# Stores of the triangles and of their 16x16 inverses issued by GpSimd's queue instead of SP's, in a two-layer hybrid decoder kernel

## The chip, the cores and the metric

The kernel runs on one core of one Trainium2 chip. The metric is the device time of one execution in microseconds: the median of three runs before the change is 1626.77 us (1626.5 to 1631.62). The profile is of one further execution, which took 1630.86 us; its span from the first to the last instruction is 1629.1 us.

## What is computed

Two decoder layers are run on two groups that share the weights: a prompt of 512 positions and eight samples of 4 positions. The width is 1024. Each layer is

```python
h = rms_norm(x, g_mix_pre)
p_rw, p_s5, p_gdn, p_swa = split_cols(h @ w_in, PROJ_SPLITS)
mix = concat([rwkv7(p_rw), s5(p_s5), gdn(p_gdn), swa(p_swa)]) @ w_out
x = x + rms_norm(mix, g_mix_post)
f = square(relu(rms_norm(x, g_mlp_pre) @ w_up)) @ w_down        # width 4096
x = x + rms_norm(f, g_mlp_post)
```

Two of the four mixers, RWKV-7 and the gated DeltaNet, are linear recurrences with four heads of 64. For the prompt they are done in chunks of 64 positions, and each chunk needs the inverse of a 64x64 unit lower triangle, as the reference writes it for the DeltaNet:

```python
A = where(strict, bc[..., :, None] * decay * einsum('bhtd,bhjd->bhtj', kc, kc), 0.0)
U = triangular_solve(eye + A, rhs, left_side=True, lower=True, unit_diagonal=True)
```

Outputs are the two groups' activations and every mixer's final state.

## The kernel before, in words

**Halves.** All columns (512 prompt positions and 32 sample positions) are cut into two halves, 0 with 256 columns and 1 with 288. `body` runs the stages for one half beside those of the other: while the mixers of one half run, the projection or the MLP of the other half supplies TensorE with large matmuls.

**Weights.** Every weight is read once per half. A weight unit is 128 output columns; `load_part` (L1675 to 1690) loads half a unit, 256 KB, from DRAM into `wraw` (five buffers) on SP's queue, at L1681. ScalarE rounds it to `whi` (L232), VectorE makes the remainder `wlo` (L236), and TensorE runs twelve matmuls on the two (L220). There are 752 such loads.

**Triangles.** A half has 256 prompt positions, so four chunks in each of four heads: 16 triangles of 64x64 for each of the two mixers, held in one tile `lt` of 128 partitions x 8 x 64 (tile class `t` for RWKV, `g` for the DeltaNet in the trace's names). `tri_begin` starts their inversion and `tri_end` ends it; a call handles the 16 triangles of one mixer, one half and one layer, and is called a triangle from here on. There are eight calls, in pairs (RWKV first, then DeltaNet).

`tri_begin` (L274 to 319) works through DRAM, because the 16x16 diagonal blocks must lie in 64 partitions, one block each:

1. two stores of `lt`, 64 partitions each, to a scratch `trsc` (L283), 64 x 8 runs of 64 floats;
2. one load of the diagonal blocks from `trsc` to `g`, tile class `c` (L286), on SP;
3. GpSimd clears a tile and sets its diagonal (L292, 293); VectorE inverts the 64 blocks with some 20 small multiplications and reductions (L300 to 312) and copies the transposed result (L313);
4. for the inverse and its transpose: one store to the DRAM array `diag` (L316), 64 x 16 runs of 16 floats, and two loads, 64 partitions each, into the tiles `t16t` and `t16` (L318), on SP.

`tri_end` then does six groups of 64x64 matmuls on TensorE, beginning with `lt` against `t16` (ps<-t,t for RWKV, ps<-t,g for the DeltaNet), and grows the 16x16 inverses to 64x64.

**Order.** The kernel is written with a tile framework: `TileContext(nc, schedule_with_timeline_sim=True)`. The framework orders the instructions of all engines anew from a simulated timeline and the priorities in `PRIO` (L137), and inserts the semaphore waits. On the chip every queue is then in order: PE (TensorE), DVE (VectorE), ACT (ScalarE), POOL (GpSimd) and SP. An instruction that waits holds back all that stand behind it on its queue. SP issues all the weight loads, the loads and stores of the triangles, of the S5 tables, of the mixers' outputs (`mix`) and of the states. POOL issues the stores of the residual stream (L1672), of the states and of two S5 tables, and computes sums of squares and small copies.

Of the kernel before, what the change touches and what calls it, by code (L numbers as in the profile page):

```python
# [139 lines left out]
class K:  # L140
# [133 lines left out]
    def tri_begin(self, lt, which):  # L274


        nc = self.nc

        blocks = lambda d: d.rearrange("(m r) -> m r", m=64)[:, :1024].rearrange("m (i t) -> m i t", t=64)[:, :, 0:16]
        rows = lambda d, c: d.rearrange("(h c r) -> c h r", h=8, c=2)[c, :, :4096].rearrange("h (i t) -> i h t", t=64)  # L280
        sc = self.t([64 * 1040], "trsc", pool="dram", bufs=2)
        for c in range(2):
            self.nc.sync.dma_start(out=rows(sc, c), in_=lt[64 * c:64 * c + 64])  # L283
        gp = self.w([64, 17, 16], "c1")
        g = gp[:, 0:16]
        self.nc.sync.dma_start(out=g, in_=blocks(sc))  # L286
        t16t, t16, work = (self.w([128, 8, 64], "t2") for _ in range(3))

        tt2 = self.view(work.rearrange("p a b -> p (a b)")[0:64], [64, 2, 16, 16])
        tt = tt2[:, 0]  # L290
        tmp = self.w([64, 16, 16], "c1")
        nc.gpsimd.memset(tt, 0.0)  # L292
        nc.gpsimd.memset(tt.rearrange("p a b -> p (a b)")[:, ::17], 1.0)

        d8 = lambda a: (a.rearrange("p a b -> p (a b)")[:, 0:272].rearrange("p (h r) -> p h r", h=2)[:, :, 0:128]
                        .rearrange("p h (c j) -> p h c j", c=8)[:, :, :, 0:8])
        t8, g8 = d8(tt2.rearrange("p x c j -> p (x c) j")), d8(gp)
        tm8 = tmp.rearrange("p a b -> p (a b)")[:, 0:128].rearrange("p (h c j) -> p h c j", h=2, c=8)
        for r in range(1, 8):
            self.tt(tm8[:, :, 0:r, 0:r], t8[:, :, 0:r, 0:r],  # L300
                    g8[:, :, 0:r, r].unsqueeze(2).to_broadcast([64, 2, r, r]))
            self.red(t8[:, :, 0:r, r], tm8[:, :, 0:r, 0:r], negate=True)

        ww = self.w([64, 8, 8], "c0")
        t4 = tmp.rearrange("p a b -> p (a b)").rearrange("p (c i j) -> p c i j", c=4, i=8)
        for c in (0, 4):
            self.tt(t4, tt[:, c:c + 4, 0:8].unsqueeze(2).to_broadcast([64, 4, 8, 8]),
                    g[:, 0:8, 8:16].rearrange("p j i -> p i j").unsqueeze(1).to_broadcast([64, 4, 8, 8]))
            self.red(ww[:, c:c + 4], t4)
            self.tt(t4, ww[:, c:c + 4].unsqueeze(2).to_broadcast([64, 4, 8, 8]),  # L310
                    tt[:, 8:16, 8:16].rearrange("p i r -> p r i").unsqueeze(1).to_broadcast([64, 4, 8, 8]))
            self.red(tt[:, c:c + 4, 8:16], t4, negate=True)
        nc.vector.tensor_copy(tt2[:, 1].rearrange("p j c -> p c j"), tt)  # L313
        for x, t in enumerate((t16t, t16)):
            d = self.diag[which][x]
            self.nc.sync.dma_start(out=blocks(d), in_=tt2[:, x])  # L316
            for c in range(2):
                self.nc.sync.dma_start(out=t[64 * c:64 * c + 64], in_=rows(d, c))  # L318
        return lt, t16, t16t, work
# [1741 lines left out]
```

## Time and profile before

| what | value |
|---|---|
| median of 3 runs | 1626.77 us |
| profiled execution / its span | 1630.86 / 1629.1 us |
| PE busy | 1555.1 us (95%) |
| DVE busy | 1195.3 us (73%) |
| ACT busy | 961.8 us (59%) |
| POOL busy | 318.0 us (20%) |
| packets of SP's queue (q1) / of POOL's (q0) | 199180 / 3744 |

Busy time is the time in which an engine executes an instruction; an engine's waits are told by another view, by line, by what released it, in total, in number and the longest. DMAs appear twice: as the time that the issuing queue needs for the instruction, and as the time from issue to landing.

### The profile page before, as it was taken

The page shows a single profiled execution, that of the slowest core. Times are in us where ns is not written, and L with a number is a line of the kernel's source. Part 1 is how long each engine was busy: PE and PEld are TensorE (multiplying, and loading weights), DVE is VectorE, ACT ScalarE, POOL GpSimd, SP SyncE. Part 2 cuts the span into 40 slices and gives each one's busy share as a digit, 9 for nine tenths or more (in the row PEclk, how much of TensorE's full clock was granted, in tenths as well). Part 3 has the DMA queues.
Part 4 walks back from the last instruction along what each step waited for, and adds up shares of the span by engine and source line. Part 5 has one row for each costly group of instructions (what it writes and reads, how often), then busy time and mean ns, then how long its engine had stood idle before and what let it go on. Part 6 is the DMA issues. An engine that isn't in the chain of part 4 may idle for free. (4 is left out here: it accounts for less than half of the span.)

```text
span 1629.1 us, 38773 instructions
## 1 busy us (share of the span) xinstructions
PE 1555.1 (95%) x14528; PEld 1453.4 (89%) x14528; DVE 1195.3 (73%) x2843; ACT 961.8 (59%) x2086; POOL 318.0 (20%) x618
## 2 busy tenths in 40 slices
PE   7989989899999999899999999999999999999996
PEld 7978978689889999888989999989888889999996
DVE  6898786976876867787595567879679755856665
ACT  6766648643455567765454467886444556755544
POOL 4751251000310428100020002620013001200001
PEclk9999999999999999999999999999999999999998
DMA  7645444443566565535365555535436655655552
GB/s 232 200 114 136 143 134 148 109 130 114 173 211 201 171 204 204 182 112 139 105 217 173 167 161 197 180 109 151 138 121 208 205 193 185 210 189 166 163 170 101
DMA packets 203112, 267.38 MB, mean 164 GB/s; under 512 B 81114, under 2 KB 95772, under 8 KB 202508
## 3 DMA queue, kind: packets, MB, share of 16 engines
q1 hardware_dynamic: 199180, 249.94, 48.9%
q0 software_dynamic: 3744, 14.96, 2.5%
q8 instruction: 114, 1.87, 0.5%
q14 instruction: 74, 0.61, 0.1%
HBM read 237.95 MB, written 28.58 MB: 164 GB/s over the span
## 5 line engine op out<-in xcount | busy, mean ns | idle before, releaser
L232 ACT CAST whi<-wraw 128x512 fp32r<-128x512 f32 x752 | 462.6, 619 | 419.2 <-PE ps L220 264.7
L236 DVE TENSOR_TENSOR wlo<-wraw,whi 128x512 fp32r<-128x512 f32 x752 | 534.9, 716 | 209.2 <-ACT whi L232 188.0
L220 PE MATMUL ps<-h,whi 128*128 128x288 f32 (+1 forms) x3264 | 519.5, 297 | 8.4 <-ACT h L228 4.4
L220 PEld LDWEIGHTS ps<-h,whi 128*128 128x128 f32 x3264 | 451.3, 191 | 25.8 <-ACT h L228 6.0
L220 PE MATMUL ps<-f,whi 128*128 128x288 f32 (+1 forms) x2752 | 421.9, 292 | 5.9 <-ACT whi L232 5.8
L220 PEld LDWEIGHTS ps<-f,whi 128*128 128x128 f32 x2752 | 372.0, 189 | 17.1 <-ACT whi L232 7.4
L220 PE MATMUL ps<-h,wlo 128*128 128x288 f32 (+1 forms) x1632 | 285.9, 295 | 5.4 <-DVE wlo L236 5.1
L220 PEld LDWEIGHTS ps<-h,wlo 128*128 128x128 f32 x1632 | 235.8, 191 | 12.3 <-DVE wlo L236 7.8
L220 PE MATMUL ps<-f,wlo 128*128 128x288 f32 (+1 forms) x1376 | 235.8, 292 | 1.7 <-DVE wlo L236 1.7
L220 PEld LDWEIGHTS ps<-f,wlo 128*128 128x128 f32 x1376 | 195.9, 189 | 5.3 <-DVE wlo L236 2.9
L236 POOL TENSOR_TENSOR sums<-sums,d 128x288 f32<-128x288 f32 (+1 forms) x54 | 51.2, 948 | 519.0 <-ACT d L228 517.7
L220 PE MATMUL ps<-r,r 64*64 64x64 f32 (+7 forms) x1184 | 67.8, 236 | 12.7 <-POOL r L236 3.8
L236 DVE TENSOR_TENSOR acc<-acc,ps 128x256 f32<-128x256 f32 (+1 forms) x96 | 41.7, 435 | 49.8 <-PE ps L220 49.7
L220 PEld LDWEIGHTS ps<-r,r 64*64 64x64 f32 (+4 forms) x1184 | 55.9, 140 | 23.2 <-issue 5.9
L232 ACT CAST f<-d 128x288 fp32r<-128x288 f32 (+1 forms) x128 | 53.3, 417 | 35.3 <-DVE d L236 35.3
L228 ACT ACTIVATE d<-ps 128x288 f32<-128x288 f32 (+1 forms) x152 | 59.8, 393 | 8.1 <-PE ps L220 6.1
L236 DVE TENSOR_TENSOR f<-d,f 128x288 fp32r<-128x288 f32 (+1 forms) x128 | 56.7, 443 | 7.4 <-ACT f L232 7.4
L236 DVE TENSOR_TENSOR d<-d 128x288 f32<-128x288 f32 (+1 forms) x128 | 56.7, 443 | 0.0
L228 ACT ACT_TABLE_LOAD x43 | 55.2, 1283 | 0.8
L220 PEld LDWEIGHTS ps<-t,t 64*64 64x64 f32 x1024 | 32.5, 135 | 4.7 <-issue 1.1
L220 PE MATMUL ps<-t,t 64*64 64x64 f32 x1024 | 36.3, 220 | 0.3 <-DMA t<-diag 0.2
L232 ACT COPY r<-ps 64x128 f32<-64x128 f32 (+2 forms) x56 | 20.4, 369 | 26.4 <-PE ps L625 11.6
(404 smaller groups left out, 1851.6 us busy)
## 6 DMA issues: line engine op xcount, KB each, us to landing
wraw<-in_w_up SPq DMA_DIRECT2D x256, 256.0 KB, 2.8
wraw<-in_w_down SPq DMA_DIRECT2D x256, 256.0 KB, 2.9
wraw<-in_w_in SPq DMA_DIRECT2D x176, 256.0 KB, 3.0
wraw<-in_w_out SPq DMA_DIRECT2D x64, 256.0 KB, 3.2
t<-diag SPq DMA_DIRECT2D x32, 128.0 KB, 3.2
x<-acc POOLq DMA_DIRECT2D x3, 1152.0 KB, 6.8
x<-acc POOLq DMA_DIRECT2D x3, 1024.0 KB, 6.4
xs<-mix SPq DMA_DIRECT2D x8, 288.0 KB, 2.9
```

The source lines that it names most:

```text
L220: return self.nc.tensor.matmul(out=out, lhsT=lhsT, rhs=rhs, start=start, stop=stop)
L228: return self.nc.scalar.activation(out=out, in_=in_, func=func, scale=scale, bias=bias, **kw)
L232: return self.nc.scalar.copy(out, in_)
L236: return (eng or self.nc.vector).tensor_tensor(out=out, in0=a, in1=b, op=op)
```

## The change

In `tri_begin`, both kinds of stores are issued by GpSimd's queue. The loads that read them back (L286, L318) stay on SP. That is 32 DMAs of an execution: 16 at L283 and 16 at L316.

```diff
         sc = self.t([64 * 1040], "trsc", pool="dram", bufs=2)
         for c in range(2):
-            self.nc.sync.dma_start(out=rows(sc, c), in_=lt[64 * c:64 * c + 64])
+            self.nc.gpsimd.dma_start(out=rows(sc, c), in_=lt[64 * c:64 * c + 64])
         gp = self.w([64, 17, 16], "c1")
...
             d = self.diag[which][x]
-            self.nc.sync.dma_start(out=blocks(d), in_=tt2[:, x])
+            self.nc.gpsimd.dma_start(out=blocks(d), in_=tt2[:, x])
             for c in range(2):
```

## Rows read from the trace of the kernel before

**Rows 1.** The page's first part: busy us, share of the span, instructions
```profile
PE 1555.1 (95%) x14528; PEld 1453.4 (89%) x14528; DVE 1195.3 (73%) x2843; ACT 961.8 (59%) x2086; POOL 318.0 (20%) x618
```
**Rows 2.** Busy by stretch: bounds, length, five engines, PE clock, DMA share, GB/s
```profile
95.00:165.00 70.00, 64.39 (x663) 56.50 (x663) 60.27 (x200) 44.76 (x130) 17.81 (x47) 0.93 0.49 129
295.00:360.00 65.00, 58.37 (x630) 48.41 (x630) 55.49 (x166) 38.12 (x94) 1.90 (x4) 0.97 0.48 126
715.00:775.00 60.00, 59.55 (x661) 53.34 (x660) 48.13 (x158) 33.49 (x89) 0.00 (x0) 1.00 0.56 149
1110.00:1170.00 60.00, 59.80 (x697) 54.34 (x697) 48.11 (x150) 33.55 (x90) 0.55 (x1) 1.00 0.60 162
```
**Rows 3.** Waits of SP's queue, whole span: total us, times, longest us
```profile
SPq L1681 <- DVE wlo L236: 704.8, 489, 6.1
...
SPq L316 <- DVE t L248: 31.4, 7, 11.8
...
SPq L318 <- DMA diag<-t: 11.1, 11, 2.8
SPq L283 <- DVE t L236: 10.4, 4, 6.4
```
**Rows 4.** ScalarE's waits on weight DMAs, third and fourth stretch (715, 1110)
```profile
ACT whi L232 <- DMA wraw<-in_w_up: 1.8, 1, 1.8
...
ACT whi L232 <- DMA wraw<-in_w_down: 2.3, 3, 1.5
```
**Rows 5.** TensorE's waits for split weights, whole span
```profile
PE ps L220 <- ACT whi L232: 8.1, 8, 2.9
PE ps L220 <- DVE wlo L236: 6.8, 12, 1.7
```
**Rows 6.** The tile trsc: issue ns min/median/max, first and last start
```profile
L283 SPq DMA_DIRECT2D trsc<-t x8: 596/624/628, 103.3 to 1114.3; - x8
```
**Rows 7.** The tile diag, the same columns
```profile
L316 SPq DMA_DIRECT2D diag<-t x16: 574/596/1430, 126.4 to 1156.8; - x16
L1842 POOL DMA_DIRECT2D diag<-r x4: 539/540/582, 69.9 to 71.6; - x4
```
**Rows 8.** DMA issues: queue, count, KB each, median us to landing
```profile
trsc<-t SPq DMA_DIRECT2D x8, 128.0 KB, 2.7
...
diag<-t SPq DMA_DIRECT2D x16, 64.0 KB, 2.8
...
out_swk_p<-sx POOLq DMA_DIRECT2D x2, 64.0 KB, 1.9
...
out_rw_p<-rwS POOLq DMA_DIRECT2D x4, 32.0 KB, 4.6
```
**Rows 9.** Line L1206 on POOL, issue ns min/median/max
```profile
L1206 POOL DMA_DIRECT2D out_swk_s<-c x2: 680/683/686, 495.9 to 1311.6; - x2
```
**Rows 10.** TensorE in order of time: first uses of inverses
```profile
133.57 0.33 PE L220 MATMUL ps<-t,t 64*64 64x64 f32 x2
...
164.48 0.73 PE L220 MATMUL ps<-t,g 64*64 64x64 f32 x17
...
327.64 0.33 PE L220 MATMUL ps<-t,t 64*64 64x64 f32 x2 [0.16 <-DMA t<-diag]
```
**Rows 11.** VectorE's waits for the read-back, third and fourth stretch
```profile
DVE c L236 <- DMA c<-trsc: 2.2, 1, 2.2
...
DVE c L236 <- DMA c<-trsc: 1.7, 1, 1.7
```
**Rows 12.** SP's queue in order of time: start us, us, line
```profile
128.89 2.86 SPq L318 DMA_DIRECT2D t<-diag  x4
...
299.22 1.29 SPq L283 DMA_DIRECT2D trsc<-t  x2
```
**Rows 13.** POOL in order of time, idle time before it and its releaser
```profile
309.78 0.90 POOL L1672 DMA_DIRECT2D x<-acc  x1 [16.22 <-ACT f L228]
```
**Rows 14.** Line L313, ns min/median/max
```profile
L313 DVE COPY t<-t x8: 374/382/395, 127.6 to 1156.1; 64x256 f32<-64x256 f32 x8
```

## The prediction

> **What bounds the kernel now.** I read the page's first part, then the four stretches in which triangles are inverted, then the waits of SP's queue, then who waits on what those queues carry. TensorE is busy for 1555.1 of 1629.1 us [rows 1], so it is the bound, and a change counts only by what it does to TensorE's 74 idle us. There are eight triangles, in four pairs (one RWKV, one DeltaNet each), and the pairs lie in the stretches 95 to 165, 295 to 360, 715 to 775 and 1110 to 1170 us. Subtract PE's busy time from the length of each: 5.6, 6.6, 0.45 and 0.2 us idle [rows 2]. So in the first two the mixers' chains starve TensorE a little, and in the last two it is full.
>
> SP's queue is in order. Its largest wait is the harmless one: 704.8 us in which a weight load waits for a buffer that VectorE has not yet released (the load is early) [rows 3]. The waits that the change touches are small beside it: 31.4 us where the store of an inverse (L316) waits for VectorE's reduction, 10.4 us where the store of a triangle (L283) waits for its masking, and behind these 11.1 us where the reading load L318 waits for the inverse's store to land [rows 3]. All this time the weight loads behind them are held up. Does anybody miss them? ScalarE, which splits each weight tile first, waits on weight DMAs for 1.8 us in the third stretch and 2.3 us in the fourth [rows 4]; in the first two stretches the same view has no such row at all. Over the whole span TensorE waits 8.1 us for a split half (whi) and 6.8 us for the other (wlo), whatever the cause [rows 5].
>
> **The change part by part.**
>
> *Issue time leaves SP.* 16 triangle stores at 0.62 us [rows 6] and 16 inverse stores at 0.596 us [rows 7] are 19.5 us of SP's sequencer. SP spends hundreds of us waiting for buffers, so this is hidden. What it can return is bounded above by the 1.8 + 2.3 = 4.1 us of ScalarE's waits for weights in the stretches, and below by nothing. I take -2 us.
>
> *The waits do not leave SP.* The loads L286 and L318 stay on SP and need the store's landing, which comes after what L283 and L316 wait for now. On an in-order queue the 31.4 and 10.4 us therefore reappear at L318 and L286, as waits on a DMA instead of on VectorE; only weight loads that the new order places between store and load gain. I cost this at 0. It would cost if POOL were late, which is the next item.
>
> *Stores issued by POOL.* A triangle store has 64 x 8 runs of 64 floats: 512 runs of 256 B. An inverse store has 64 x 16 runs of 16 floats: 1024 runs of 64 B. By the shapes in the code no DMA that POOL issues now has more than one run per partition, so 128. The nearest rows: 128 runs (the zero fill, L1842) take 0.54 us each on POOL [rows 7], and 32 runs (L1206) 0.68 us [rows 9]. So between 32 and 128 runs there is no slope, but both lie far below 512. Bounds: flat, 0.54 us for each; or in proportion to runs, 0.54 x 4 = 2.2 us and 0.54 x 8 = 4.3 us. The rows decide for neither end where it matters, so I take the geometric middle, 1.1 and 1.5 us. Stores come in twos, so until the second one is issued: triangle 2.2 us against 1.25 on SP (+0.9), inverse 3.1 against 1.2 (+1.9).
>
> *Landing.* SP's stores land 2.7 and 2.8 us after issue; small stores of POOL between 1.9 and 4.6 us [rows 8], middle 3.2. That is +0.4 us each way; bounds -0.9 and +1.8. Together a triangle's read-back comes 1.3 us later and an inverse's 2.3 us later.
>
> *Who notices.* For the RWKV triangle of each pair TensorE reaches the first matmul on the inverse (ps<-t,t, two matmuls) just as it has landed: at 133.57 us in the first pair, 1.8 us after SP was through with the four loads (128.89 + 2.86) [rows 10, 12], and after a wait of 0.16 us on that DMA in the second [rows 10]; the other two pairs repeat it. So there is no slack on TensorE's in-order queue in four of eight triangles. The DeltaNet inverse of the first pair is first used at 164.48 [rows 10], 31 us after the RWKV one, while VectorE works on its triangle right behind the other's. I count no exposure for these four, which is a choice: without slack they would add up to 4 x 2.3 us. VectorE already waits 2.2 and 1.7 us for a triangle's read-back in the third and fourth stretch [rows 11], so no slack there either; in the first two stretches there is no such row. Sum: third and fourth pair, where TensorE has no idle time to give, 2 x (2.3 + 1.3) = 7.2 us; first and second pair 2 x 2.3 = 4.6 us, of which I count half, because the delay partly falls on the 5.6 and 6.6 us that are idle anyway: 2.3. That is +9.5, less the 2 us returned: +7.5 us.
>
> *What POOL holds up.* In the last three stretches POOL is busy for 1.9, 0 and 0.55 us [rows 2], so its 32 new instructions delay nothing of weight. In the first it is busy for 17.8 us with small copies that the projection of the other half needs; four triangle and four inverse stores add 4 x 1.1 + 4 x 1.5 = 10.4 us to that, in a stretch with 52 us of room. I cost it at 0, up to 4 us if the copies queue behind a waiting store.
>
> *A rule that speaks against it.* After the last reduction VectorE copies the inverse in 0.38 us, once per triangle [rows 14], exactly when the first inverse store is due. The Trainium skill, SBUF — State Buffer, section "Who interferes with whom", says that a VectorE copy in its two-port mode shuts GpSimd out, descriptor writing for DMAs included, until it ends. No row here shows a POOL DMA held that way. By it the sum would be 4 x 0.38 = 1.5 us higher, since four inverses have no slack; without it, as I leave it.
>
> The profiled execution took 1630.86 us, its span 1629.1 and 1.8 us around it; by the sum it would be 1638.4. It lies 4.1 us above the median of 1626.77, so against the median of the runs the forecast is 1626.8 + 7.5 = 1634 us.
>
> **The rivals.**
>
> *Flat price, nothing happens.* At 0.54 us a store and +0.4 us landing, the third and fourth pair lose 2 x 0.8 and the others half of 2 x 0.4: +2.0, less 2: 1627 us (1625 with the full 4.1 returned). For it: the rows from 32 to 128 runs. Against it: 512 and 1024 runs are untested. The Trainium skill, DMA: Bandwidth & Descriptors, section "Anatomy of one DMA", puts descriptor generation at "small, variable" and says that many descriptors can be emitted before their cost shows; by that rule this rival is what happens, and the two rows agree as far as they go.
>
> *Price in proportion to runs.* Triangle stores +3.1 and inverses +7.4, with landing 3.5 and 7.8 us: 2 x (7.8 + 3.5) + 7.8 = 30.4, less 2: 1655 us. For it: back-to-back zero fills are 0.54 us apart, as if 128 runs took that long. Against it: 32 runs take no less, and an order of work computed anew may put other matmuls ahead of the late ones.
>
> *The other side: weights come earlier.* The order of every queue is computed anew with SP freed of the stores. If weight loads fill the gap between store and read-back, the splits run ahead, and TensorE's 8.1 + 6.8 = 14.9 us of waits for whi and wlo shrink; half of them gone gives 1619, all 1612 us. It decides from the point where TensorE's waits for the two fall under 8 us while the RWKV inverses cost less than 1 us each. For it: the held-up SP. Against it: ScalarE misses weights for only 4.1 us in these stretches, and most of the 14.9 us lies elsewhere.
>
> *A store stuck on POOL.* POOL too is in order, and the store of the residual (L1672) is held there for 16.2 us, until 309.78 [rows 13], while the second pair's triangle store goes out from SP at 299.22 [rows 12]. If the store stands behind it, it leaves 10.6 us late. Some 3 us of that is slack before VectorE needs it, so VectorE stalls about 7.5 us, and the time is 1634 to 1642 with the forecast's other terms. Against it: an order by due times puts the earlier one first.
>
> **How the numbers follow.** Forecast (middle price) 0.35, flat 0.25, weights earlier 0.20, proportional 0.13, stuck store 0.07. The likeliest one's own range, from landing and price around the middle, is 1628 to 1642. The overall range reaches to the proportional case (1655, cut a little for its low chance) and into the faster one: 1615 to 1653. A measurement of this kernel tells no change from about 0.3%, 4.9 us: 1621.9 to 1631.7. Slower: three quarters of the forecast, the proportional and nearly all of the stuck case, 0.45. Same: four fifths of the flat case, a fifth of the forecast and of the faster one, 0.33. Faster: 0.22.
>
> **What would show it.** Right: the POOL rows of L283 and L316 between 1 and 2 us; SP's waits at L316 and L283 gone and those at L318 and L286 grown by about as much; TensorE waiting 2 us and more on t<-diag at the RWKV inverses; PE idle grown in the third and fourth stretch. Wrong: POOL rows at 0.54 or above 4 us; TensorE's waits on t<-diag unchanged; or idle time that changes outside the four stretches, which would say that the new order of the work, and not the stores, made the difference.

## The result and the profile after

The changed kernel takes 1650.34 us (median of 4 runs, 1648.7 to 1654.62), the kernel before on the same chip 1629.19 (4 runs, 1626.5 to 1635.82): ratio 1.0116, interval 1.009 to 1.0142. It is slower by about 19 us. The profiled execution took 1650.15 us with a span of 1648.4, so 19.3 us more than the span of before.

The page's first part of the changed kernel, the answer to [rows 1]:

```profile
PE 1570.2 (95%) x14528; PEld 1466.1 (89%) x14528; DVE 1200.4 (73%) x2843; ACT 960.0 (58%) x2086; POOL 346.2 (21%) x650
```

TensorE executes the same 14528 matmuls, but is busy for 15.1 us longer; its idle time grows by only 4.2 us (78.2 against 74). So most of the loss is not waiting at all: the same work runs more slowly. The next rows say why.

Busy time by stretch of the changed kernel, the answer to [rows 2]: the four stretches with triangles (their bounds moved with the weight units around them), and the piece of the second in which the clock is low (columns as there; the figure after the engines is PE's granted clock):

```profile
95.00:165.00 70.00, 63.78 (x623) 56.00 (x622) 61.03 (x201) 45.03 (x127) 27.82 (x59) 0.93 0.47 127
300.00:372.00 72.00, 64.97 (x658) 55.00 (x659) 60.22 (x181) 39.14 (x100) 8.12 (x12) 0.86 0.43 111
727.00:791.00 64.00, 63.77 (x685) 57.47 (x685) 53.54 (x172) 35.13 (x96) 6.74 (x10) 1.00 0.53 150
1126.00:1190.00 64.00, 63.47 (x723) 57.69 (x724) 51.17 (x154) 35.33 (x93) 7.20 (x11) 1.00 0.56 160
...
302.50:319.60 17.10, 14.32 (x82) 10.68 (x79) 16.16 (x52) 10.00 (x21) 3.70 (x5) 0.50 0.30 75
```

In the third and fourth stretch, where the forecast put most of its loss, TensorE is idle for 0.23 and 0.53 us, as before (0.45 and 0.2). The second has a granted clock of 0.86 (0.97 before), because it is 0.50, the lower of the two levels (1.2 of 2.4 GHz), for 17.1 us at a stretch. Before, the only low piece of that stretch is 3.4 us.

What the low level costs is read from equal matmuls. TensorE in order of time, kernel before (start, us, operation), the same kind of group at the high and at the low level:

```profile
85.59 1.10 PE L220 MATMUL ps<-h,whi 128*128 128x256 f32 x8
...
104.54 2.16 PE L220 MATMUL ps<-h,whi 128*128 128x256 f32 x8
```

Twice as long. So about half of TensorE's busy time at the low level is lost. Cut the span at the clock's changes, take busy and idle time of each piece, and the run splits into three terms, here from the start to the last of the 752 splits of a weight (wlo), in which both kernels execute 14491 matmuls. Busy time of the two kernels in exactly that window (before first):

```profile
0.00:1610.95 1610.95, 1549.27 (x14491) 1448.46 (x14492) 1187.62 (x2834) 957.20 (x2079) 315.08 (x616) 0.99 0.52 165
```
```profile
0.00:1630.20 1630.20, 1564.40 (x14491) 1461.20 (x14492) 1192.76 (x2833) 955.42 (x2079) 343.31 (x648) 0.98 0.51 163
```

Idle is length minus busy: 61.7 before, 65.8 after. TensorE is busy at the low level for 35.8 us before and 68.1 after, so half is 17.9 and 34.0. The rest is 1531.3 and 1530.4: the same. The difference of 19.3 us is 4.1 of idle time, 16.1 of low clock and -0.9. These are the terms of one execution of each kernel. The clock of the other executions says the same: granted over the whole span it is 0.972 to 0.975 in the four of the changed kernel, and 0.977 to 0.988 in the 23 of the kernel before that stand beside the first experiment.

Where the time is lost is read from the starts of the 752 splits. From here on, and in the expectations below, a weight unit is one of these 752 half-unit loads. Busy time between the starts of the splits of the 82nd and the 144th, before and after:

```profile
238.50:430.83 192.33, 182.10 (x2003) 159.88 (x2005) 143.31 (x412) 109.95 (x250) 21.90 (x45) 0.98 0.43 127
```
```profile
236.09:447.34 211.25, 197.13 (x2095) 173.25 (x2092) 149.61 (x434) 110.94 (x257) 36.57 (x81) 0.91 0.40 121
```

The changed kernel begins this stretch about level (2.4 us ahead at this split, 0.2 behind at the next) and leaves it some 15 us behind (16.5 at this split, 14.7 at the next), of the 19.3 at the end. The two orders place the splits differently, so a delay read at a single split is good to a few microseconds: around the first pair it swings between 3 us ahead and 5 behind. A part of the loss, 1 to 5 us, lies before the second pair's first store.

The stores themselves, lines on POOL with issue ns min/median/max, changed kernel, the answer to [rows 6, 7]:

```profile
L283 POOL DMA_DIRECT2D trsc<-t x8: 707/730/791, 104.9 to 1131.5; - x8
L283 POOL DMA_DIRECT2D trsc<-g x8: 700/700/754, 118.2 to 1134.1; - x8
...
L316 POOL DMA_DIRECT2D diag<-t x16: 833/833/875, 129.9 to 1177.8; - x16
```

Their landing (queue, count, KB each, median us), the answer to [rows 8]:

```profile
trsc<-t POOLq DMA_DIRECT2D x8, 128.0 KB, 2.8
trsc<-g POOLq DMA_DIRECT2D x8, 128.0 KB, 4.8
diag<-t POOLq DMA_DIRECT2D x16, 64.0 KB, 3.2
```

Waits of the changed kernel (total us, times, longest): SP's queue, the answer to [rows 3]; then TensorE's, the answer to [rows 5]:

```profile
SPq L1681 <- DVE wlo L236: 757.1, 492, 8.1
...
SPq L318 <- DMA diag<-t: 20.4, 10, 5.4
...
SPq L286 <- DMA trsc<-t: 8.0, 3, 7.2
...
SPq L286 <- DMA trsc<-g: 6.2, 4, 3.1
```
```profile
PE ps L220 <- DVE wlo L236: 9.0, 11, 2.2
PE ps L220 <- ACT whi L232: 7.6, 7, 3.1
...
PE ps L220 <- DMA t<-diag: 2.0, 2, 1.5
```

SP no longer waits at L283 and L316; it waits at the two loads instead. TensorE waits for a read-back twice, 2.0 us in all. Nothing here accounts for 19 us. What did change on a large scale is the order: the framework computed a new one, and 4775 of the 11906 places on TensorE's queue hold another instruction than before.

### The profile page after: what moved, and what is told of

Same layout as the page of the kernel before. It is cut to its first block, busy times and chain, and to the rows that moved or that the text cites. A ratio compares the mean times of both kernels' runs of the same rounds, so it can differ in the third digit from the quotient of the medians.

```text
span 1648.4 us, 38794 instructions
## 1 busy us (share of the span) xinstructions
PE 1570.2 (95%) x14528; PEld 1466.1 (89%) x14528; DVE 1200.4 (73%) x2843; ACT 960.0 (58%) x2086; POOL 346.2 (21%) x650
## 5 line engine op out<-in xcount | busy, mean ns | idle before, releaser
L236 DVE TENSOR_TENSOR wlo<-wraw,whi 128x512 fp32r<-128x512 f32 x752 | 532.1, 713 | 215.5 <-ACT whi L232 183.4
L220 PE MATMUL ps<-h,wlo 128*128 128x288 f32 (+1 forms) x1632 | 290.4, 298 | 6.6 <-DVE wlo L236 6.2
L220 PEld LDWEIGHTS ps<-h,wlo 128*128 128x128 f32 x1632 | 239.1, 193 | 14.2 <-DVE wlo L236 9.4
L236 POOL TENSOR_TENSOR sums<-sums,d 128x288 f32<-128x288 f32 (+1 forms) x54 | 52.4, 970 | 508.1 <-ACT d L228 507.8
L236 DVE TENSOR_TENSOR acc<-acc,ps 128x256 f32<-128x256 f32 (+1 forms) x96 | 41.7, 434 | 58.8 <-PE ps L220 58.8
L236 DVE TENSOR_TENSOR f<-d,f 128x288 fp32r<-128x288 f32 (+1 forms) x128 | 56.8, 444 | 5.2 <-ACT f L232 4.9
L236 DVE TENSOR_TENSOR d<-d 128x288 f32<-128x288 f32 (+1 forms) x128 | 57.6, 450 | 0.3 <-ACT d L228 0.3
```

What stands on the lines that cost most here:

```text
L220: return self.nc.tensor.matmul(out=out, lhsT=lhsT, rhs=rhs, start=start, stop=stop)
L236: return (eng or self.nc.vector).tensor_tensor(out=out, in0=a, in1=b, op=op)
```

## The experiments

Theory ORDER: the newly computed order of all queues makes the loss, and which queue issues the stores hardly matters. Theory QUEUE: the late stores make it. In all runs a ratio is to the kernel before on the same chip.

**The two halves of the change, taken apart.** An order is taken over whole by chaining each engine's instructions in a recorded sequence with dependencies that only the framework's ordering sees, no new semaphores (shortened; the kernel unpacks the sequence from a table):

```diff
-        K(tc, ctx, ins, outs).body()
+        K(tc, ctx, ins, outs).body(); pin(tc)
+def pin(tc):
+    for ins in recorded_order:
+        if ins.engine in last:
+            tc.add_manual_dep(ins, last[ins.engine].name, K.NOSYNC, reason="pin")
+        last[ins.engine] = ins
```

With the change (stores on POOL) in the order of before:

> The 32 stores go to POOL, but every queue keeps the order of work of the kernel before (each store stands on POOL where it stood in that order; SP's loads close up). Theory QUEUE (the stores' way over POOL is what costs: its in-order waits and its longer issue): ratio 1.008 to 1.015, TensorE's waits on t<-diag above 4 us. Theory ORDER (the order of work that was computed anew is what costs, the queue is nearly free): ratio 0.998 to 1.003, the second pair's 17 us at low clock gone.

Measured: 1635.18 us against 1633.95, ratio 1.0017, interval 1.0001 to 1.0034. TensorE waits 2.0 us for t<-diag in all, and the long piece at the low clock in the second pair's stretch is gone (6.8 us is the longest there). And the mirror, stores on SP in the order of the changed kernel:

> The 32 stores stay on SP, but every queue has the order of work of the changed kernel (each store stands on SP where it stood in that order). QUEUE: ratio 0.998 to 1.003. ORDER: ratio 1.008 to 1.015, with the same loss of some 16 us between 245 and 430 us and the same long stretch at low clock in the second pair.

Measured: 1653.26 us, ratio 1.0108, interval 1.0088 to 1.0128. The new order alone, with no store moved, gives nearly all of 1.0116. First part of the page, the store-moving run and then the order-moving run:

```profile
PE 1559.8 (95%) x14528; PEld 1456.6 (89%) x14528; DVE 1198.5 (73%) x2843; ACT 961.4 (59%) x2086; POOL 347.7 (21%) x650
```
```profile
PE 1570.1 (95%) x14528; PEld 1466.7 (89%) x14528; DVE 1199.7 (73%) x2843; ACT 959.3 (58%) x2086; POOL 320.4 (19%) x618
```

POOL's busy time follows the stores, TensorE's the order: 1559.8 in the old one, 1570.1 in the new. ORDER holds. The old order pinned with the stores on SP was not run; that the pinned new order comes out as the unpinned one (1.0108 and 1.0116) says that pinning itself costs little.

**One kind of store alone, with a new order each.** First only L283 as in the change, then only L316.

```diff
-            self.nc.sync.dma_start(out=rows(sc, c), in_=lt[64 * c:64 * c + 64])
+            self.nc.gpsimd.dma_start(out=rows(sc, c), in_=lt[64 * c:64 * c + 64])
```

> Only the 16 triangle stores (L283) go to POOL, order computed anew. QUEUE: the two halves of the cost add up, so about a third to a half of the loss, ratio 1.003 to 1.007. ORDER: this is another new order, so the ratio has nothing to do with a share of the change: anywhere from 0.99 to 1.015, and the loss need not lie in the second pair.

Measured: 1643.2 us, 1.006 (1.0036 to 1.0083).

```diff
-            self.nc.sync.dma_start(out=blocks(d), in_=tt2[:, x])
+            self.nc.gpsimd.dma_start(out=blocks(d), in_=tt2[:, x])
```

> Only the 16 inverse stores (L316) go to POOL, order computed anew. QUEUE: the larger part of the loss, ratio 1.005 to 1.010, so that this and the triangles' run add up to 1.0116. ORDER: again a new order, anywhere from 0.99 to 1.015, and the two do not add up to 1.0116.

Measured: 1637.77 us, 1.0021 (1.0008 to 1.0034). The triangles' ratio lies in both theories' ranges, that of the inverses only in ORDER's. The two don't say which store is dear: they are a third and a fourth order.

**Where the new order loses.** Stores on POOL; the recorded order is a splice, cut at the 82nd and the 144th weight unit (the diff tells in code how the recorded table was made):

```diff
-recorded_order = before
+recorded_order = before[:u82] + sorted(before[u82:u144], key=place_in_after) + before[u144:]
```

> Stores on GpSimd's queue. Every queue is pinned to the order of the kernel before, except between the 82nd and the 144th weight unit (about 240 to 431 us, the stretch around the second pair of triangles), where it has the order of the changed kernel. Theory SECOND PAIR (nearly all of the loss is made by the new order in this one stretch): ratio 1.007 to 1.011, some 12 to 17 us, with over 75 us at the low level of TensorE's clock. Rival SPREAD (the new order loses a little everywhere and the milestones only show it first here): 1.002 to 1.005, hardly above the 1.0017 of the fully old order. Rival PREFIX (the state at 240 us, which the new order before it left, is what makes the stretch slow): 1.002 to 1.004, low level near 53 us.

Measured: 1647.81 us against 1632.72, 1.0088 (1.0068 to 1.0108), as SECOND PAIR said; the low level lasted 72.7 us in the profiled execution, a little under its 75. The splice the other way round (names exchanged):

```diff
-recorded_order = after
+recorded_order = after[:u82] + sorted(after[u82:u144], key=place_in_before) + after[u144:]
```

> The mirror of the run above: stores on GpSimd's queue, every queue in the order of the changed kernel, except between the 82nd and the 144th weight unit, where it has the order of the kernel before. SECOND PAIR: ratio 1.001 to 1.004, and 55 us or so at the low clock. SPREAD: 1.007 to 1.010. PREFIX: 1.007 to 1.011, with the 302 to 320 us stretch still at the low clock.

Measured: 1642.19 us, 1.0061 (1.004 to 1.0081), between what SECOND PAIR and SPREAD had said. PREFIX is out: the longest low piece there is 6.8 us, not 17. So this stretch makes some 0.0055 to 0.007 of the loss (1.0116 - 1.0061, and 1.0088 - 1.0017), and the order elsewhere the other 0.003 to 0.0045; each of these ratios is sure to about 0.002 only. The stretch itself, as the busy view cuts it, stores on POOL: old order, and new order only there (nearly the same work, 2003 and 2014 matmuls):

```profile
239.62:433.79 194.17, 185.25 (x2003) 162.80 (x2005) 143.63 (x412) 109.97 (x250) 28.65 (x52) 0.96 0.44 126
```
```profile
238.56:439.64 201.08, 189.79 (x2014) 166.80 (x2016) 144.80 (x412) 108.06 (x249) 28.33 (x53) 0.92 0.41 121
```

6.9 us longer: idle 11.3 against 8.9 (+2.4), and busy 26.0 us at the low clock against 13.3 (half of the difference is 6.4; the rest falls by 1.8). This profiled execution was the fastest of its six, 7 us below their median, so it shows less of the loss than the ratio does. What happens at the fall, TensorE in order of time, new order only there:

```profile
294.02 1.16 PE L220 MATMUL ps<-r,r 64*128 64x128 f32 x16
...
298.34 1.11 PE L220 MATMUL ps<-cst,gdlb 128*64 128x128 f32 x16 [1.88 <-DVE gdsc L236]
299.38 1.03 PE L220 MATMUL ps<-e,mean 128*128 128x256 f32 x2
300.35 3.09 PE L220 MATMUL ps<-r,r 64*128 64x128 f32 x16
```

and in the old order, where the sixteen r,r of 300.35 come three to five microseconds earlier, in three groups between other work and close behind weight matmuls (h,whi):

```profile
293.03 1.10 PE L220 MATMUL ps<-h,whi 128*128 128x256 f32 x8
294.06 1.09 PE L220 MATMUL ps<-cst,gdlb 128*64 128x128 f32 x12
295.07 0.71 PE L220 MATMUL ps<-r,r 64*128 64x128 f32 x4
...
296.34 0.71 PE L220 MATMUL ps<-r,r 64*128 64x128 f32 x4
...
297.34 1.16 PE L220 MATMUL ps<-r,r 64*128 64x128 f32 x8
```

(The names are those of the mixers' small tiles; gdsc and gdlb belong to the DeltaNet.) In the new order TensorE waits 1.88 us for VectorE, then has small groups only, and the clock falls to 0.50 at 299.6 for 13.7 us; sixteen r,r take 3.09 us, where an equal group six microseconds earlier, at the high level, took 1.16. That this wait makes the clock fall is the sequence seen here, not something that a run isolated.

**Orders that no store has asked for.** Two nudges of the framework's priorities on the kernel before, and the same two on the changed kernel:

```diff
-PRIO = {..., 'gd1': 200, ..., 'load': 294, ...}
+PRIO = {..., 'gd1': 200, ..., 'load': 290, ...}    # first; second: 'gd1': 190, 'load': 294
```

> No store is moved: the kernel before with the priority of the weight loads in the planner at 290 instead of 294, which makes it compute another order (3337 of 11906 places on TensorE's queue change, about as many as in the experiments that moved one kind of store). Theory DRAW (any newly computed order falls at random, and the order of before is a good draw): ratio between 0.998 and 1.012, more likely above 1.002 than not. Rival GUIDED (the new order is bad because the planner was told that the stores are on GpSimd's queue): 0.998 to 1.002.

Measured: 1661.82 us, 1.017 (1.0148 to 1.0192): slower than even DRAW had allowed (1.012).

> As the run above, by another neutral nudge: the priority of the DeltaNet's first section at 190 instead of 200 (3189 of 11906 places on TensorE's queue change). DRAW: 0.998 to 1.012, and not the same as the run above. GUIDED: 0.998 to 1.002, the same as the run above.

Measured: 1646.31 us, 1.008 (1.0062 to 1.0098).

> The changed kernel (all stores on GpSimd's queue) with the priority of the weight loads in the planner at 290 instead of 294; 3519 of 11906 places on TensorE's queue differ from the order of the changed kernel. Theory DRAW (the time of a newly computed order is set by the order, hardly by which queue issues the stores): anywhere between 0.998 and 1.02, and not near 1.0116 but by accident; the twin of this nudge with the stores on SP came out at 1.017. Rival GUIDED (orders computed with the stores on GpSimd's queue are bad because of these stores): 1.009 to 1.014, as the changed kernel. Span minus PE idle minus half of the busy time at the low clock: 1526 to 1533 us by the accounting of the runs so far.

Measured: 1658.42 us against 1633.38, 1.0156 (1.0138 to 1.0174).

> The changed kernel with the priority of the DeltaNet's first section at 190 instead of 200; 2735 of 11906 places on TensorE's queue differ from the order of the changed kernel. DRAW: 0.998 to 1.02, another value than the run above; the twin with the stores on SP was 1.008. GUIDED: 1.009 to 1.014. The same accounting: 1526 to 1533 us.

Measured: 1644.94 us, 1.0072 (1.0054 to 1.009). A nudge of one priority by 1.4 or 5% costs about as much as the change under study, and the same nudge comes out the same on either queue, within the intervals. GUIDED is out by the two runs with no store moved: it had said at most 1.002. DRAW is shown only in part: orders differ this much whatever the queue, but that each nudge costs the same twice does not look like a fresh draw. Nor is it shown that the nudges are neutral. The priorities before (294, 392, 5486) are not round; if they were chosen by measured time, other values would lose on the average, and no run tells. First part of the page, load at 290, stores on SP, then on POOL:

```profile
PE 1573.3 (95%) x14528; PEld 1470.2 (89%) x14528; DVE 1202.7 (73%) x2843; ACT 963.9 (58%) x2090; POOL 316.2 (19%) x618
```
```profile
PE 1572.5 (95%) x14528; PEld 1469.9 (89%) x14528; DVE 1204.3 (73%) x2843; ACT 963.9 (58%) x2090; POOL 346.3 (21%) x650
```

**An order edited by hand.** If the order is worth so much, can the old one be bettered at its two largest idle times (A and B), and at two smaller places (D and E, left out of the excerpt below)?

```diff
 recorded_order = before
+move_before([gdsc, gdsc, masks of ps344 and ps345], f<-f,g)      # A, DVE, 97 us
+move_before([gdsc, whi, e<-ps], d<-acc)                          # A, ACT
+move_before([e<-ps, whi], r<-r)                                  # B, ACT, 235 us
+move_before(wlo, e<-ps,g)                                        # B, DVE
...
```

> Stores on SP and the order of the kernel before, with four places edited by hand, each so that an instruction that was ready no longer stands behind one that waits: (A) at 97 us the gdsc chain and the RWKV masks ahead of the 2.11 us f<-f,g on DVE, and whi, e and gdsc ahead of d on ACT (there PE had been idle for 3.95 us, with 6.8 us at the low clock behind it); (B) at 235 us the copy e<-ps ahead of r on ACT and the next wlo ahead of e<-ps,g on DVE (PE idle 5.15 us, and 6.8 us at the low clock); (D) at 835 us four matmuls ahead of the eight r,r that wait for POOL; (E) at 314 us the softmax's reciprocal ahead of the triangle's multiplications on DVE. Theory ORDER WITH CLOCK (span = about 1530 us of matmuls at full clock + PE idle + half of the busy time at the low clock): idle falls by 7 to 10 us and the low-clock time by up to 13 us, ratio 0.990 to 0.997. Rival GIVEN BACK (PE then waits for the next thing and nothing remains): 0.998 to 1.003.

Measured: 1637.41 us against 1633.12, 1.0032 (1.0015 to 1.005): slower, where ORDER WITH CLOCK had said faster.

> The same hand-edited order with the triangles' stores on GpSimd's queue. If the queue itself costs what it did in the pinned order of before (ratio 1.0017), this run is 0.1 to 0.3% above the run with the stores on SP. QUEUE HELPS (SP's freed 20 us count once PE's larger waits are gone): equal or faster.

Measured: 1642.7 us, 1.0058 (1.0035 to 1.008), 0.26% above its twin. TensorE in order of time, kernel before at the two places, then the hand-edited order on SP:

```profile
101.20 2.00 PE L220 MATMUL ps<-cst,gdlb 128*64 128x128 f32 x16 [3.95 <-DVE gdsc L236]
...
239.58 0.85 PE L220 MATMUL ps<-e,cst 128*128 128x288 f32 x1 [5.15 <-ACT e L232]
```
```profile
97.94 1.11 PE L220 MATMUL ps<-cst,gdlb 128*64 128x128 f32 x16 [1.07 <-DVE gdsc L236]
...
104.47 0.65 PE L220 MATMUL ps<-f 64*64 64x128 f32 x8 [1.79 <-ACT g L228]
...
236.19 0.75 PE L220 MATMUL ps<-e,cst 128*128 128x288 f32 x2 [0.49 <-ACT e L232]
...
242.26 0.75 PE L220 MATMUL ps<-e,cst 128*128 128x288 f32 x2 [2.13 <-ACT e L232]
...
249.58 3.75 PE L220 MATMUL ps<-r,r 128*128 128x256 f32 x8 [3.46 <-DMA r<-s5sz]
```

Both waits shrink as meant (3.95 to 1.07 and 5.15 to 0.49), and TensorE then waits for the next thing: 1.79 at 104, 2.13 at 242, 3.46 for an S5 read-back at 249.58. The clock falls there in turn, at 105.5 and 248.8 us, for 6.8 us each. At the 78th weight unit the kernel is 0.3 us ahead, at the 90th 3.4 us behind; around edit D, at 835 us, another 3.6 are lost, with 6.8 us at the low clock. Idle time falls by 3.5 us in all, and the low-clock term rises by 9.6. GIVEN BACK, and more. No version that ran beats the kernel before.

All profiles in the three terms, up to the last wlo (us; low clock is half of the busy time at 0.50). The ratio is that of all executions, the terms are those of the one that was profiled:

| kernel | ratio | idle | low clock | rest |
|---|---|---|---|---|
| before | 1 | 61.7 | 17.9 | 1531.3 |
| changed | 1.0116 | 65.8 | 34.0 | 1530.4 |
| old order, POOL | 1.0017 | 61.3 | 21.5 | 1532.5 |
| new order, SP | 1.0108 | 64.2 | 34.6 | 1529.7 |
| triangles only / inverses only on POOL | 1.006 / 1.0021 | 68.8 / 66.6 | 26.2 / 19.4 | 1529.0 / 1532.1 |
| new order in the second pair only / all but there | 1.0088 / 1.0061 | 61.9 / 61.9 | 28.7 / 27.1 | 1530.0 / 1531.5 |
| load 290, SP / POOL | 1.017 / 1.0156 | 72.6 / 73.0 | 41.3 / 38.2 | 1526.3 / 1528.4 |
| gd1 190, SP / POOL | 1.008 / 1.0072 | 64.2 / 66.2 | 37.3 / 32.6 | 1527.4 / 1527.0 |
| hand order, SP / POOL | 1.0032 / 1.0058 | 58.2 / 64.0 | 27.5 / 29.3 | 1530.8 / 1529.5 |

The rest stays within 1526 to 1533 us; idle time and low clock, which the order sets, carry most of every large difference. The rest is lowest where the low clock is long (1526.3 at 41.3), so half may charge the low level somewhat too much; and differences of a few microseconds, as between the first and the third row, are within what the executions of one kernel differ by.

## Why the prediction was right and wrong

The direction was right and the time lay inside the range, but most of the loss came by a road that the prediction had not priced. That it lay inside is luck: 1650 us is above the forecast's own 1628 to 1642, in the part of the range that was there for a price in proportion to the runs, and the stores refuted that price.

*The bound.* TensorE is the bound, right. The step that failed is the next half sentence, "a change counts only by what it does to TensorE's 74 idle us": of the 19.3 us only 4 are idle time and 16 are the same matmuls at the low clock. The view by stretch had the granted clock in it [rows 2], and it was read only for idle time.

*What a new order is worth.* The prediction saw that every queue is ordered anew, and used it only in the rival on the other side, as a gain. Orders newly computed, on either queue, cost between 0.2 and 1.7% in the seven kernels run (the changed one, each kind of store alone, four nudges); none was as good as the order of before. This term, 1.0108, is where the missing size lies. The prediction's last clause, that changes outside the four stretches would say that the order made the difference, is what happened: the loss begins at 245 us, ahead of the second pair's stretch, and 3 of the 4.1 us of new idle time lie outside the four stretches.

*Issue time leaves SP*: 19.5 us left it, and nothing of the 2 us shows. TensorE's waits for whi and wlo are 16.6 us against 14.9 [rows 5], in the old order with POOL's stores 15.5.

*The waits do not leave SP*: right. SP's waits at L286 before, which the prediction left out, then those at L318 and L286 in the old order with POOL's stores:

```profile
SPq L286 <- DMA trsc<-t: 4.3, 4, 1.9
SPq L286 <- DMA trsc<-g: 4.1, 5, 1.6
```
```profile
SPq L318 <- DMA diag<-t: 47.0, 9, 15.7
...
SPq L286 <- DMA trsc<-t: 16.5, 5, 10.4
...
SPq L286 <- DMA trsc<-g: 10.1, 5, 3.1
```

So the 41.8 us that vanished at L283 and L316 reappear: 73.6 us at the two loads against 11.1 [rows 3] and 8.4, 54.1 more. In the changed kernel's own order they are 34.6 us.

*The price of a store*: taken as 1.1 and 1.5 us, measured 0.70 to 0.73 for 512 runs and 0.83 for 1024. With 0.54 for 128 [rows 7] the bound "flat" was much nearer than "in proportion", and nearer than the middle that the forecast took. The Trainium skill, DMA: Bandwidth & Descriptors, section "Anatomy of one DMA", calls descriptor generation "small, variable"; these rows agree, and the flat rival, which followed from it, was the nearest for the price.

*Landing*: +0.4 us predicted; +0.4 for the inverses (3.2), +0.1 for the RWKV triangles (2.8), and 1.4 for the DeltaNet ones (4.8 against 3.4 before; 3.9 in the old order with POOL's stores).

*Who notices*: mis-sized. The forecast charged 7.2 us to the third and fourth pair. TensorE waits there for a read-back once, 0.5 us, and 1.5 us in the second pair; VectorE's waits for trsc are 4.2 us against 3.9. The exposure that was foreseen is best read in the old order with POOL's stores, where only the queue differs: TensorE waits for t<-diag once in each pair, 0.3 to 0.9 us, 2.0 in all against 0.2 before, where late read-backs were to cost +9.5, and its idle time does not grow (61.3 against 61.7). At the same order the move of the queue cost +0.17% (old order, 0.01 to 0.34) and +0.26% (hand-edited, where the two intervals overlap), some 3 and 4 us where +7.5 was forecast. In the new order it is +0.08%, against two different sets of runs of the kernel before, which is no difference.

*What POOL holds up*: nothing that shows. Idle time of the first stretch is 6.2 us against 5.6.

*The rivals.* Flat price came nearest for the stores (1627, no change) and was wrong on the total, because it too left the order out. By the Trainium skill, SBUF — State Buffer, section "Who interferes with whom", a VectorE copy in its two-port mode shuts out descriptor writing. That is not seen in the changed kernel: its sixteen L316 rows lie between 0.833 and 0.875 us. Whether the copy of L313 runs in that mode no trace says. One such row of the old-order run took 1.18 us, at 345.55; the copy came after it, at 346.99, and VectorE ran multiplications meanwhile (L242, L236), so it was not the copy. What the traces do show is the copy itself taking longer. Line L313 in the changed kernel and in the old-order run, ns min/median/max (374/382/395 before [rows 14]):

```profile
L313 DVE COPY t<-t x8: 378/382/532, 131.0 to 1175.7; 64x256 f32<-64x256 f32 x8
```
```profile
L313 DVE COPY t<-t x8: 374/381/729, 127.9 to 1162.3; 64x256 f32<-64x256 f32 x8
```

The two long ones, at 327.20 and 149.33, are those that began well inside the issue of a store on POOL (0.48 and 0.30 us after its start, stores of 0.84 us). So there the copy was late by 0.15 and 0.35 us and the store was not; that the store held it up is the overlap seen in two cases, not something that a run isolated.

Left open: why the framework's orders lose to the one of before, and what in a stretch brings TensorE's clock down; only the sequence of wait and fall was seen.

## What to carry to other kernels

Where a framework orders the queues anew, an edit is two changes: what it does, and a new order. Take them apart by pinning the order before explaining anything by the edit, and run a neutral nudge or two to see how far an order alone moves the time; here that spread (0.8 and 1.7%) is about as large as the change under study (1.2%). Read a busy TensorE with its granted clock: split the time into idle, half of the busy time at the low level, and rest, and see which of the three moved.

## What the runs showed of the hardware

GpSimd's software queue moves the same bytes in far fewer packets, as the trace counts them. Queues, packets, MB and share of the engines' time, changed kernel:

```profile
q1 hardware_dynamic: 174092, 246.80, 46.7%
q0 software_dynamic: 5024, 18.11, 3.7%
```

SP's queue loses 25088 packets for the 32 stores (they have 24576 runs), and GpSimd's gains 1280, 40 a store. Packets under 512 B fall from 81114 to 56539. The issue time on POOL hardly follows the runs: 0.54 us for 128, 0.70 to 0.73 for 512, 0.83 for 1024.
